# Queries of a head loaded one piece of work ahead into three tiles of each kind; operands of later stages made in a pool of four tiles

## The chip, the cores and the metric

One core of a Trainium2 chip. The metric is the device time of one execution of the whole program in microseconds (us), from one launch. TensorE (PE, with its weight loads PEld) multiplies, VectorE (DVE), ScalarE (ACT) and GpSimd (POOL) do the element-wise work, and SyncE (SP) issues every DMA of this kernel, in the order of its queue.

## What is computed

One layer on 2048 tokens of width 1024: a projection to queries, keys and values, two kinds of attention (8 heads with a forgetting gate over all earlier keys, 8 heads over a band of nine chunks of 64 tokens with a learned bias), an output product, a layer norm, a feed-forward block with a causal convolution, and a second norm. Cut to what matters here:

```python
def token_mixer(x, w_in, b_forget, rel_bias, w_out):
    proj = x @ w_in
    q_a, k_a, v_a, f_a, q_b, k_b, v_b = jnp.split(proj, SPLITS, axis=-1)
    log_f = jax.nn.log_sigmoid(f_a + b_forget).transpose(0, 2, 1)
    y_a = forgetting_attention(split_heads(q_a, 8), split_heads(k_a, 8), split_heads(v_a, 8), log_f)
    y_b = chunked_band_attention(split_heads(q_b, 8), split_heads(k_b, 8), split_heads(v_b, 8), rel_bias)
    y = jnp.concatenate([y_a, y_b], axis=1).transpose(0, 2, 1, 3).reshape(b, s, D_MIX)
    return y @ w_out

def reference(x, ...):
    x = layer_norm(ALPHA * x + token_mixer(x, w_in, b_forget, rel_bias, w_out), ln1_g, ln1_b)
    return layer_norm(ALPHA * x + conv_ffn(x, w_up, conv_w, conv_b, w_down), ln2_g, ln2_b)
```

All inputs are float32. The kernel keeps that precision by splitting an operand into a high part in the fast matmul format (`hi`) and a remainder (`lo`) and doing three matmuls for each product (`mm3`, lines 184 to 186).

## The kernel before

**Order.** The kernel is written against a tile framework: the Python code emits instructions in a program order, and a scheduler then places them on the engines, by that order as priority and by its own idea of when operands are ready. Every engine runs its list strictly in order, SP too: a DMA whose wait is not over holds all DMAs behind it.

**Stages.** First the projection alone (`projection`, products accumulated in `acc`, lines 184 to 186; call this dense work). Then attention and the rest of the projection woven together (`weave`): after each attention step, dense units are emitted in a fixed ratio. Before a pair of heads `p` is started, `ready(p)` emits dense units until its group of projections is complete. There are two attention passes, tokens 0 to 1023 (`chunks` 0 and 1) and tokens 1024 to 2047 (chunks 2 and 3); the dense work goes on with the output product of the first tokens. The rest, the feed-forward products, follows.

**Attention.** A piece of work is (pair of heads p, head s, chunk c of 512 queries), 32 in each pass, 64 in all. `start(n)` loads its keys (`load_keys`: tiles `ka`, `kb`, `vv`) and returns the generator `maxima`, whose first act before the change is to load the queries: `qa` (pool `a_q`, 2 buffers) and one of the two fixed tiles `qb0`, `qb1` (list `QB`), three DMAs (lines 552 to 554). `maxima` multiplies queries by keys (`sc`, line 574), DVE reduces each product to a row maximum (lines 577 and 582), and the maxima go back into row 96 of `qb` (line 592, ACT). `logits` then multiplies again (`st`, lines 611 and 612), ACT takes the exponential (`pt`, line 623), POOL adds up the rows (line 632), and `weigh` multiplies by the values (`y`, line 698). `sc` and `st` have two PSUM banks each. In the loop over work, item i's logits are interleaved with item i+1's maxima: `start(i + 1)` is called at the top of item i.

**Operands of later stages.** `prepare_weights` makes hi and lo parts of `w_out` (16 operands, `wo_d`) and of seven sums or differences of blocks of `w_down` for each of 11 row blocks (77 operands, `wd_d`; 55 of them combine two blocks), and stores them to DRAM for later. It is a generator that `dense_work` advances one step every `PRE` = 9 dense units, from unit 60 on. Before the change a group first loads its four source blocks (`w_raw0` to `w_raw3`, one buffer each), then makes its operands one by one in one tile `w_hl` (both parts, one buffer): DVE combines into the lo half where two blocks are needed (line 279), ACT copies the hi part (line 177), DVE subtracts (line 180), one DMA stores both parts, 512 KB (line 282). The next operand may write `w_hl` only when that store has landed.

## Time and profile before

| what | value |
|---|---|
| times of three runs | 2785.5, 2792.08 and 12486.5 us; median 2792.08 us |
| profiled execution | 2789.79 us, span 2788.0 us from the first to the last instruction |
| PE busy | 2724.5 us, 98% of the span, 12632 matmuls |
| DVE, ACT, POOL busy | 1941.7, 1160.7, 623.2 us (70%, 42%, 22%) |
| mean granted clock of PE | 0.993 |
| bytes moved by DMA | 527.40 MB |

How to read it: a stretch is limited by the engine that is never idle there, and what a change can give is found in the idle time of that engine, and in what ended it. Granted clock 1.0 is the 2.4 GHz level, 0.5 the 1.2 GHz one; a value between them is the mean over a stretch in which both occurred. The third run above (12486.5 us) is far from the other two.

### The profile page before, as it was taken

The page shows a single profiled execution, that of the slowest core. Times are in us where ns is not written, and L with a number is a line of the kernel's source. Part 1 is how long each engine was busy: PE and PEld are TensorE (multiplying, and loading weights), DVE is VectorE, ACT ScalarE, POOL GpSimd, SP SyncE. Part 2 cuts the span into 40 slices and gives each one's busy share as a digit, 9 for nine tenths or more (in the row PEclk, how much of TensorE's full clock was granted, in tenths as well). Part 3 has the DMA queues.
Part 4 walks back from the last instruction along what each step waited for, and adds up shares of the span by engine and source line. Part 5 has one row for each costly group of instructions (what it writes and reads, how often), then busy time and mean ns, then how long its engine had stood idle before and what let it go on. Part 6 is the DMA issues. An engine that isn't in the chain of part 4 may idle for free.

```text
span 2788.0 us, 38642 instructions
## 1 busy us (share of the span) xinstructions
PE 2724.5 (98%) x12632; PEld 2045.3 (73%) x12632; DVE 1941.7 (70%) x3577; ACT 1160.7 (42%) x2004; POOL 623.2 (22%) x754
## 2 busy tenths in 40 slices
PE   9999999999999999999998999999999999999998
PEld 7676767675666656766786888888887788888886
DVE  4557576777677655668568888876568877777559
ACT  4434444444444443433225555553222555544221
POOL 2235242327567555333000000000000000000000
PEclk9999999999999999999999999999999999999999
DMA  8666767665455444677894444428778222236974
GB/s 242 197 207 196 228 194 229 211 201 169 144 182 182 137 144 153 199 198 217 293 328 142 141 166 156 155 83 311 260 247 322 87 80 81 78 88 206 323 227 161
DMA packets 324618, 527.40 MB, mean 189 GB/s; under 512 B 70688, under 2 KB 86176, under 8 KB 324416
## 3 DMA queue, kind: packets, MB, share of 16 engines
q1 hardware_dynamic: 324416, 524.93, 59.1%
q8 instruction: 100, 1.64, 0.2%
q14 instruction: 102, 0.84, 0.1%
HBM read 362.65 MB, written 162.14 MB: 188 GB/s over the span
## 4 chain that ended last, share of the span: by engine, by line
PE 84%; DVE 4%; DMA 4%; ACT 1%; issue 1%; POOL 0%; SPq 0%; DVEq 0%; ACTq 0%; POOLq 0%
PE acc L184 21%; PE acc L186 21%; PE acc L185 21%; PE y L698 8%; PE st L611 4%; PE sc L574 4%; PE st L612 3%; DMA qb<-qh_d 1%; PE sc L650 1%; DVE slot L180 1%; DVE slot L1132 1%; DMA slot<-in_w_v_dram 1%; DMA wd_d<-w_hl 1%; PE acc L841 0%; DVE slot L816 0%
## 5 line engine op out<-in xcount | busy, mean ns | idle before, releaser
L184 PE MATMUL acc<-slot,slot 128*128 128x512 f32 (+2 forms) x3064 | 1165.7, 381 | 17.9 <-ACT slot L177 17.9
L186 PE MATMUL acc<-slot,slot 128*128 128x512 f32 (+2 forms) x3064 | 1160.5, 379 | 6.6 <-DVE slot L180 6.6
L185 PE MATMUL acc<-slot,slot 128*128 128x512 f32 (+2 forms) x3064 | 1161.3, 379 | 0.0
L177 ACT ACTIVATE slot<-slot 128x512 fp32r<-128x512 f32 (+1 forms) x680 | 416.4, 626 | 674.2 <-DVE slot L1121 193.0
L184 PEld LDWEIGHTS acc<-slot,slot 128*128 128x128 f32 x3064 | 580.4, 189 | 135.9 <-ACT slot L177 23.5
L186 PEld LDWEIGHTS acc<-slot,slot 128*128 128x128 f32 x3064 | 579.7, 189 | 126.2 <-DVE slot L180 10.8
L185 PEld LDWEIGHTS acc<-slot,slot 128*128 128x128 f32 x3064 | 580.4, 189 | 112.6 <-issue 2.8
L180 DVE TENSOR_TENSOR slot<-slot,slot 128x512 fp32r<-128x512 f32 (+1 forms) x652 | 450.7, 707 | 194.4 <-ACT slot L177 167.9
L632 POOL TENSOR_TENSOR sums<-sums,pt 128x512 f32<-128x512 f32 (+3 forms) x416 | 426.0, 1024 | 251.9 <-ACT pt L623 189.0
L623 ACT ACTIVATE pt<-st 128x512 f32<-128x512 f32 (+3 forms) x544 | 261.7, 492 | 333.4 <-PE st L612 121.4
L698 PE MATMUL y<-pt,vv 128*64 128x512 f32 (+3 forms) x1088 | 281.6, 505 | 0.2 <-DVE yt L640 0.2
L611 PE MATMUL st<-qa,ka 128*128 128x512 f32 (+2 forms) x544 | 209.0, 385 | 9.0 <-ACT pt L623 8.5
L574 PE MATMUL sc<-kb,qb 66*128 66x512 f32 (+2 forms) x544 | 186.6, 373 | 10.8 <-DMA qb<-qh_d 8.1
L612 PE MATMUL st<-qb,kb 97*128 97x512 f32 (+2 forms) x544 | 189.9, 357 | 4.4 <-ACT qb L592 3.9
L577 DVE TENSOR_REDUCE mx<-sc 128x1 f32<-128x512 f32 x192 | 127.9, 686 | 80.0 <-PE sc L574 78.3
L611 PEld LDWEIGHTS st<-qa,ka 128*128 128x128 f32 x544 | 103.0, 189 | 96.0 <-issue 44.1
L698 PEld LDWEIGHTS y<-pt,vv 128*64 128x64 f32 x1088 | 82.0, 136 | 124.2 <-issue 111.5
L574 PEld LDWEIGHTS sc<-kb,qb 66*128 66x128 f32 x544 | 99.5, 190 | 78.6 <-DVE mx L582 17.5
L856 DVE SCALAR_TENSOR_TENSOR v<-u,cw,v 128x1024 f32<-128x1024 f32 x88 | 113.0, 1285 | 62.4 <-ACT v L855 44.2
L1005 POOL COPY u<-halo 128x2 f32<-128x2 f32 x44 | 17.6, 401 | 620.8 <-DVE v L857 620.8
L582 DVE CUSTOM_DVE_ANT_0 junk<-sc,bq 128x512 bf16<-128x512 f32 (+2 forms) x224 | 108.2, 483 | 49.4 <-PE sc L574 40.2
L632 POOL TENSOR_TENSOR sums<-pt 128x384 f32<-128x384 f32 (+1 forms) x64 | 79.5, 1243 | 255.4 <-PE sc L650 181.4
(116 smaller groups left out, 2250.3 us busy)
## 6 DMA issues: line engine op xcount, KB each, us to landing
slot<-wd_d SPq DMA_DIRECT2D x308, 256.0 KB
slot<-in_w_up_dram SPq DMA_DIRECT2D x176, 256.0 KB
wd_d<-w_hl SPq DMA_DIRECT2D x77, 512.0 KB
slot<-wo_d SPq DMA_DIRECT2D x128, 256.0 KB
h_d<-v SPq DMA_DIRECT2D x44, 512.0 KB
slot<-h_d SPq DMA_DIRECT2D x88, 256.0 KB
slot<-in_w_qk_dram SPq DMA_DIRECT2D x66, 256.0 KB
xq_d<-slot SPq DMA_DIRECT2D x56, 256.0 KB
```

Of the source, the lines that this page charges most:

```text
L177: nc.scalar.activation(hi, src, AF.Copy)
L180: lo_eng.tensor_tensor(lo, src, f32(hi), op=ALU.subtract)
L184: nc.tensor.matmul(acc, wh, mh, start=first, stop=False, **more)
L185: nc.tensor.matmul(acc, wh, ml, start=False, stop=False, **more)
L186: nc.tensor.matmul(acc, wl, mh, start=False, stop=last, **more)
L574: nc.tensor.matmul(sc[:, m0:m1], qb[:KR, tq], kb[:KR, m0:m1], start=True, stop=True)
L577: nc.vector.tensor_reduce(m, sc[:, k0:k1], axis=AX.X, op=ALU.max)
L611: nc.tensor.matmul(st[:, w2], ka[:, js], qa[:, w2], start=True, stop=False)
L612: nc.tensor.matmul(st[:, w2], kb[:KM, js], qb[:KM, w2], start=False, stop=True)
L623: nc.scalar.activation(pt[:, w], st[:, w], AF.Exp)
L632: nc.gpsimd.tensor_tensor(acc[:, w], (acc if first is None else first)[:, w], pt[:, w], op=ALU.add)
L698: nc.tensor.matmul(y[half, w], v, pt[:, w], start=first and n < 2, stop=last and n >= len(tiles) - 2)
```

## The change

Queries are loaded by a function of their own, `load_queries(n)`, called in `start` for work n and for work n+1, so for one piece ahead; `qa` has three buffers and there are three `qb` tiles, taken in turn by n. `load_queries` calls `ready` too, so the projections of a group of heads are completed one piece of work earlier. `prepare_weights` loses its four source tiles and `w_hl`. It now takes an operand at a time: load into `w_lo` (2 buffers), load a second block into `w_v` (1 buffer) where there is one, a `yield`, combine in place, ACT copies hi to `w_hi` (1 buffer), DVE subtracts in place, two stores of 256 KB, a `yield`. Source blocks that several operands use are loaded once for each. `PRE` goes from 9 to 5, since an operand now takes two steps.

```diff
-PRE0, PRE = 60, 9
+PRE0, PRE = 60, 5
...
-        def parts(dst, u, v=None, op=None):
-            hl = tl(pool, [P, 2, CH], F32R, "w_hl")
+        def rows(src, i, j):
+            return src[i * P : i * P + P, CH * j : CH * j + CH]
+
+        def operand(dst, u, v=None, op=None):
+            lo, hi = tl(pool, [P, CH], F32, "w_lo", 2), tl(pool, [P, CH], F32R, "w_hi")
+            nc.sync.dma_start(lo, u)
             if v is not None:
-                src = f32(hl[:, 1])
-                nc.vector.tensor_tensor(src, u, v, op=op)
-                u = src
-            split(hl[:, 0], hl[:, 1], u, nc.scalar, nc.vector)
-            nc.sync.dma_start(dst.rearrange("l p m -> p l m"), f32(hl))
...
+                tmp = tl(pool, [P, CH], F32, "w_v")
+                nc.sync.dma_start(tmp, v)
             yield
...
+            if v is not None:
+                nc.vector.tensor_tensor(lo, lo, tmp, op=op)
+            split(hi, lo, lo, nc.scalar, nc.vector)
+            nc.sync.dma_start(dst[0], f32(hi))
+            nc.sync.dma_start(dst[1], lo)
+            yield
...
-        yp, pp, sm, qp = pool("a_y", 1), pool("a_p", 4), pool("a_sm", 4), pool("a_q", 2)
+        yp, pp, sm, qp = pool("a_y", 1), pool("a_p", 4), pool("a_sm", 4), pool("a_q", 3)
...
-        for n in range(2):
+        for n in range(3):
             t = tl(cst, [P, CH], F32R, f"qb{n}")
...
-        def maxima(p, s, c, head, qs):
+        def load_queries(n):
+            p, s, c = work[n]
+            ready(p)
...
             qa = tl(qp, [P, CH], F32R, "qa")
-            qb = QB[steps % 2]
-            steps += 1
+            qb = QB[n % len(QB)]
             nc.sync.dma_start(f32(qa[0:HD]), ql_d[p, hs, cs])
             nc.sync.dma_start(f32(qa[HD:P]), qh_d[p, hs, cs])
             nc.sync.dma_start(f32(qb[0:HD]), qh_d[p, hs, cs])
-            qs += [qa, qb]
+            queries[n] = qa, qb
...
-            qs = []
-            return head[s], qs, maxima(p, s, c, head[s], qs)
+            for k in (n, n + 1):
+                if k < len(work) and k not in queries:
+                    load_queries(k)
+            qs = queries.pop(n)
+            return head[s], qs, maxima(p, s, c, head[s], qs[1])
```

The line numbers move a little: the three matmuls of attention, 574, 611 and 612 before, stand at 572, 609 and 610 after, the value product 698 at 699; 184 to 186 and 177 to 180 stay. What the scheduler makes of it, at three places:

**PE, seventh piece of the second pass** (queries in `qb_962` before, in `qb_975` after). Before, the first product with the new queries stands right behind a value product:

```order
L186 MATMUL acc<-slot_7583,slot_5237 128x256
L698 MATMUL y<-pt,vv 64x512
L574 MATMUL sc<-kb_956,qb_962 128x512
L574 MATMUL sc<-kb_959,qb_962 128x512
L698 MATMUL y<-pt,vv 64x384
```

and after, behind the transposes that end the maxima of the piece ahead:

```order
L186 MATMUL acc<-slot_7787,slot_5305 128x256
L589 MATMUL sc<-ident_r,nm 1x128 x4
L609 MATMUL st<-qa,ka 128x512
L572 MATMUL sc<-kb_969,qb_975 128x512
L184 MATMUL acc<-slot_7787,slot_5310 128x256
L185 MATMUL acc<-slot_7788,slot_5310 128x256
L610 MATMUL st<-qb_981,kb_957 128x512
```

The maxima of one piece now follow those of the last without a gap in the list, with dense rows and logits of the piece in work (`qb_981`) between them.

**PE, where the second attention pass begins** (its first queries are in `qb_962` before, in `qb_975` after). Before, dense rows stand between the first products:

```order
L650 MATMUL sc<-sums,ones 64x512 x2
L574 MATMUL sc<-kb_941,qb_962 128x512
L611 MATMUL st<-qa,ka 128x512
L184 MATMUL acc<-slot_5194,slot_6747 128x512
L185 MATMUL acc<-slot_5195,slot_6747 128x512
L574 MATMUL sc<-kb_944,qb_962 128x512
L186 MATMUL acc<-slot_5194,slot_6748 128x512
L611 MATMUL st<-qa,ka 128x512
```

After, a long dense stretch ends there, and the first piece's twelve products (three key tiles for each of four query blocks) stand together:

```order
L186 MATMUL acc<-slot_5310,slot_6918 128x512
L609 MATMUL st<-qa,ka 128x512
L572 MATMUL sc<-kb_954,qb_975 128x512
L572 MATMUL sc<-kb_957,qb_975 128x512
L609 MATMUL st<-qa,ka 128x512
L572 MATMUL sc<-kb_960,qb_975 128x256
L572 MATMUL sc<-kb_954,qb_975 128x512
L572 MATMUL sc<-kb_957,qb_975 128x512
L572 MATMUL sc<-kb_960,qb_975 128x256
L572 MATMUL sc<-kb_954,qb_975 128x512
L572 MATMUL sc<-kb_957,qb_975 128x512
L572 MATMUL sc<-kb_960,qb_975 128x384
```

No dense row (184 to 186) follows for 61 matmuls. Over the whole attention part, the lists hold three stretches of 40 to 42 matmuls without a dense one before, and nine stretches of 31 to 91 after (431 matmuls in all, against 124).

**SP, the operands of later stages, in the middle of the second pass.** Before, four source blocks are loaded together, and one store belongs to an operand:

```order
L282 DMA wd_d<-w_hl 128x2x512
L523 DMA vv<-v_d 128x256
L400 DMA v_d<-slot_8174 128x4x64
L288 DMA w_raw_8581<-in_w_down_dram 128x512
L288 DMA w_raw_8583<-in_w_down_dram 128x512
L288 DMA w_raw_8585<-in_w_down_dram 128x512
L288 DMA w_raw_8587<-in_w_down_dram 128x512
```

After, a load or two and two stores belong to each operand (queries of the piece ahead, `qb_975`, and a key tile, `kb_954`, stand a few rows above):

```order
L547 DMA qb_975<-qh_d 64x512
L517 DMA ka<-kh_d 64x512
L518 DMA ka<-kl_d 64x512
L510 DMA kb_954<-kh_d 64x512
L512 DMA kb_954<-cum_d 2x512
L288 DMA wd_d<-w_hi 128x512
L519 DMA vv<-v_d 128x256
L289 DMA wd_d<-w_lo 128x512
L280 DMA w_lo<-in_w_down_dram 128x512
L396 DMA v_d<-slot_8382 128x4x64
L283 DMA w_v<-in_w_down_dram 128x512
```

The lists of the feed-forward stages hold the same matmuls in the same number as before.

## Rows read from the trace of the kernel before

**Rows 1.** The page: span, and busy time of the engines.

```profile
span 2788.0 us, 38642 instructions
...
PE 2724.5 (98%) x12632; PEld 2045.3 (73%) x12632; DVE 1941.7 (70%) x3577; ACT 1160.7 (42%) x2004; POOL 623.2 (22%) x754
```

**Rows 2.** Busy time by stage: stretch, length, PE, PEld, DVE, ACT, POOL, clock, DMA.

```profile
75.00:1340.00 1265.00, 1236.16 (x6114) 839.65 (x6114) 827.09 (x1972) 534.72 (x1058) 561.68 (x590) 0.99 0.62 188
...
1510.00:2720.00 1210.00, 1204.39 (x5203) 974.99 (x5202) 897.53 (x1223) 527.26 (x776) 43.90 (x124) 1.00 0.54 176
```

**Rows 3.** PE's waits, 60 to 1340 us: total, times, longest.

```profile
PE st L611 <- ACT pt L623: 8.5, 9, 2.1
PE sc L574 <- DMA qb<-qh_d: 8.1, 8, 2.1
PE st L612 <- ACT qb L592: 3.9, 3, 2.8
...
PE sc L574 <- DVE mx L582: 2.4, 2, 1.2
```

**Rows 4.** Timeline at one such wait: start, length, engine, instruction, idle before.

```profile
752.61 0.55 SPq L554 DMA_DIRECT2D qb<-qh_d  x1
...
758.52 0.73 PE L574 MATMUL sc<-kb,qb 66*128 66x512 f32 x2 [2.13 <-DMA qb<-qh_d]
```

**Rows 5.** Stretches of 5 us around the two longest such waits, as rows 2.

```profile
115.00:120.00 5.00, 5.00 (x15) 2.75 (x15) 2.69 (x9) 0.38 (x1) 0.72 (x1) 0.66 0.57 184
...
760.00:765.00 5.00, 5.00 (x24) 4.31 (x23) 2.71 (x7) 2.63 (x5) 1.49 (x2) 0.66 0.26 80
```

**Rows 6.** The chain that ended last, near 1000 us: start, length, what.

```profile
996.45 3.05 DMA wd_d<-w_hl
...
1000.75 0.39 PE st L611
```

**Rows 7.** ACT's waits for DMAs, 60 to 1340 us (ten rows).

```profile
ACT slot L177 <- DMA slot<-in_w_qk_dram: 20.0, 15, 3.3
...
ACT w_hl L177 <- DMA wd_d<-w_hl: 9.6, 10, 2.7
...
ACT w_hl L177 <- DMA wo_d<-w_hl: 4.3, 4, 2.2
...
ACT w_hl L177 <- DMA qh_d<-slot: 2.0, 1, 2.0
...
ACT slot L177 <- DMA qh_d<-slot: 1.2, 2, 0.6
```

**Rows 8.** DVE's waits for DMAs, 60 to 1340 us (four rows).

```profile
DVE w_hl L279 <- DMA wd_d<-w_hl: 18.3, 15, 3.4
...
DVE w_hl L279 <- DMA w_raw<-in_w_down_dram: 3.3, 3, 1.7
```

**Rows 9.** SP's own waits: total, times, longest.

```profile
SPq L552 <- PE st L612: 64.6, 31, 7.9
```

**Rows 10.** Groups of DVE, 75 to 1340 us: count, busy, mean ns, idle before.

```profile
L577 DVE TENSOR_REDUCE mx<-sc 128x1 f32<-128x512 f32 x192 | 127.9, 686 | 80.0 <-PE sc L574 78.3
...
L582 DVE CUSTOM_DVE_ANT_0 junk<-sc,causal_w 128x512 bf16<-128x512 f32 x32 | 21.8, 683 | 0.5 <-PE sc L574 0.2
```

**Rows 11.** PE's four waits where the second pass begins, 580 to 616 us.

```profile
PE sc L650 <- POOL sums L632: 1.4, 1, 1.4
...
PE y L698 <- DVE yt L640: 0.2, 1, 0.2
```

**Rows 12.** PE's waits in a stretch without dense work, 335 to 350 us.

```profile
PE st L611 <- ACT pt L623: 0.6, 1, 0.6
```

**Rows 13.** DMA issues of the operands: duration of the issue (ns), first and last.

```profile
L282 SPq DMA_DIRECT2D wd_d<-w_hl x77: 359/377/1182, 208.5 to 1020.1; - x77
...
L288 SPq DMA_DIRECT2D w_raw<-in_w_down_dram x44: 327/430/1148, 176.6 to 957.7; - x44
```

**Rows 14.** The page: DMA issues by line, count and size.

```profile
slot<-in_w_qk_dram SPq DMA_DIRECT2D x66, 256.0 KB
```

More of the change, by code (lines that the diff above doesn't have):

```diff
@@ L500, in attention @@
         loads = 0
-        steps = 0
+        queries = {}
         zeros = set()
@@ L554, in maxima @@
             nc.sync.dma_start(f32(qb[0:HD]), qh_d[p, hs, cs])
-            qs += [qa, qb]
+            queries[n] = qa, qb
+        def maxima(p, s, c, head, qb):
+            fox = p < 4
+            KR = HD + 2
             seg = c + 1 if fox else min(c + 1, 2)
```

25 lines of the change are left out of this document (6 added, 19 removed).

## Prediction, made before the changed kernel ran

> **What bounds the kernel now.** I read the page first: PE is busy for 2724.5 us of a span of 2788.0, so 63.5 us of idle PE are all that better order can give [rows 1]. By stage, 1236.16 of the 1265 us between 75 and 1340 us are PE's, which leaves 28.8 us idle in the stretch in which attention and projection are woven; from 1510 to 2720 us it is 5.6 us [rows 2]. The change touches nothing behind the weave, so its whole account lies in those 28.8 us, and in what the clock costs beside them. Next I read who ended PE's waits there: the exponentials on ACT for 8.5 us, the queries' load into `qb` for 8.1 in eight waits, the row of maxima that ACT writes into `qb` for 3.9, a DVE reduction for 2.4 [rows 3]. The reader is to see two kinds: PE waits on a DMA itself, or on ACT or DVE, which were late.
>
> The timeline shows the first kind at its worst. SP issues the load of `qb` at 752.61; PE runs out of other work, waits 2.13 us, and starts with the new queries at 758.52, 5.9 us behind the issue [rows 4]. The five microseconds behind it have a granted clock of 0.66, so about two thirds of them ran at 1.2 GHz instead of 2.4, and PE lost 1.7 us (0.34 x 5) while it counts as busy; the same 0.66 stands from 115 us on, behind another of the eight [rows 5].
>
> The second kind shows in the chain. A store of `w_hl` takes 3.05 us to land, ACT holds its next operand back for it, an exponential is queued behind that, and PE gets on with the product behind it at 1000.75, 4.3 us after the issue [rows 6]. Such waits on DMAs add up to 72.7 us on ACT (ten rows) [rows 7] and 27.4 on DVE (four rows) [rows 8]: 100 us, for which PE waited at most 14.8 us on these two engines (8.5 + 3.9 + 2.4) [rows 3]. So about 15% of a wait of ACT or DVE reaches PE.
>
> All sums are against the profiled execution, 2789.8 us; the median of the runs shown is 2.3 us above it.
>
> **Queries one piece ahead.** The three DMAs and their bytes stay; they are emitted one piece earlier. SP still holds them until the piece before last has done its last product with the tile: that wait, 64.6 us in 31 times, concerns the same event as before [rows 9], and SP's queue behind it stalls as it did. But the first reader comes one piece later, 1265 us / 64 pieces, some 20 us, against 5.9 us from issue to use at the worst place. I take the 8.1 us as gone, and the two stretches of low clock with them: **-8.1 and -3.4**. The bounds: nothing gained, and this sum.
>
> What is late next: with `qb` there, the products may start as soon as the keys are, and the scheduler lets them follow the last maxima directly, as the rows of order show. Keys are now the last thing to land. The trace of before has no wait of PE for `kb`. Between 0 and the 8.1 us that `qb` cost I take **+2**, nearer to none, since the keys stand a few issues ahead of where the queries stood.
>
> **Dense work bunched.** `ready` is called a piece earlier, and PE's list has 431 matmuls in stretches without dense rows against 124. Where the second pass begins, twelve products with two PSUM banks stand together, so DVE's reductions set the pace: eight of 686 ns and, on the diagonal, four of 683 ns at most, 5.5 to 8.2 us and say 7.4 [rows 10], of which PE's own part is 12 x 0.235 = 2.8 (a 512-column dense product about every 0.23 us: 1204.39 us / 5203 in the later stage [rows 2]). The first two need not wait. That is 4 us of idle PE. Then PE waits for the maxima to come back into `qb` (2.8 us at the longest [rows 3]; products of the next piece hide part: 1), perhaps for the load of `qb` itself (0 to 2.1, the longest of the eight waits [rows 3]: 1), and the clock falls once (1.7 [rows 5]). That is 7.7 us; what PE waited there before, 3.1 us in four waits [rows 11], goes: **+4.5**, between 0 and +9. The other eight dense-free stretches have 370 matmuls; in the three of before, 124 matmuls, PE waited for ACT in one, 0.6 us [rows 12]; by their number that is 1.8, so **+2**, between 0 and +8 (8.5 us is all that PE waited for ACT's exponentials [rows 3]). Elsewhere bunching costs nothing, since PE is busy with the one or the other; if that cover went, it would be priced like these stretches.
>
> **Operands of later stages.** 153 DMAs (60 loads, 93 stores) become 334 (148 loads, 186 stores): 181 issues more at 0.38 to 0.43 us [rows 13], 69 to 78 us of SP up to 1020 us. SP is off the path while its loads are early, so this costs nothing directly; it delays what queues behind, and the price is in the waits below. The 88 loads more bring 23 MB, a tenth of what the stretch moves (188 GB/s x 1265 us = 238 MB); the DMA engines are busy 0.62 of it, so they have room [rows 2]. ACT's and DVE's instructions are the same in number (93 copies, 93 subtractions, 55 combinations).
>
> Removed: the waits for the one `w_hl` to be stored, 9.6 + 4.3 on ACT [rows 7] and 18.3 on DVE, and 3.3 for the source blocks [rows 8], with a 2.0 of ACT between: 37.5 us, of which 15% reach PE: -5.6. Added: waits for loads that now stand one operand ahead instead of up to four. Nearest is the weight load of the projection, which is split soon after its issue: 20.0 us [rows 7] for 66 loads [rows 14], 0.30 us each. 148 loads at that price are 45 us, 15% of it 6.7. Waits for `w_hi` to be stored I put at a fifth of those removed, 0.5. Together **+1.5**. The bounds: none of the new waits (-5.6), or every one straight to PE (+39).
>
> The Trainium skill, in "DMA: Bandwidth & Descriptors", section "Bandwidth", says to batch DMAs to 1 MiB or more, and in its fit gives every transfer a fixed 2.0 us beside its bytes at 436 GB/s: by it a 512 KB store would be an estimated 3.2 us and each of two halves 2.6, which speaks against this change. The 3.05 us of the store agree with the page [rows 6]; no row of before has its half.
>
> **The sum.** -8.1 - 3.4 + 2 + 4.5 + 2 + 1.5 = -1.5, so 2788.3 us on the profiled execution's 2789.8: I forecast **2788**, no change that counts. What the queries give is taken back where dense work is bunched.
>
> **The rivals.**
> First, slower: ACT is held by loads. Its place is the copy to `w_hi` (line 177) ahead of exponentials in ACT's list, with two `st` banks behind it. For it speaks that this path is on the chain already [rows 6]; against it, that only 15% of such waits arrive. At 148 loads x 0.30 us = 45 us, all of it reaching PE, less 11.5 for the queries and 5.6: 2818. It decides from the point where ACT's waits pass on more than a quarter (11 us). Over 2% (2846) it would take 0.5 us for each load, all at PE.
>
> Second, faster: the bunching is hidden, keys are early and the new waits are few: -11.5 - 5.6 = -17, 2773; with half of PE's 14.8 us on ACT and DVE gone too, 2765.
>
> Third, the change does not do what it says: SP's queue, longer by 181 issues and held 64.6 us by these very loads [rows 9], brings the queries no earlier. Then 2789.8 + 4.5 + 2 + 1.5 = 2798.
>
> Fourth, hidden slack: if busy PE is not PE at its peak, more than 63.5 us could go, and the time fall below 2734. Against it speaks that the later stage runs 5203 matmuls in 1204 us with hardly any wait [rows 2]. The Trainium skill, in "Trainium Kernel Development and Optimization", section "Performance Expectations", calls matmul busy time a bad measure of distance from peak, because matmuls are pipelined, and wants that of weight loads; by it the 73% of PEld would leave room [rows 1], but the change removes no matmul and no weight load.
>
> **How the numbers follow.** Forecast, 2778 to 2795: 0.5. Slower by held ACT, 2796 to 2845: 0.18, half of it below 2812; over 2% 0.02. Faster, 2752 to 2777: 0.18, most of it above 2770. Change without its effect, 2796 to 2805: 0.1. Hidden slack, below 2734: 0.01; the last 0.01 for a second pass that starves PE for longer (over 2%). The range 2770 to 2812 takes in the forecast, the third rival, half of the first and most of the second: 0.8. The forecast's own is 2778 to 2795. A measurement of this kernel can tell about 2% from no change (56 us), so faster 0.01, within 0.96, slower 0.03.
>
> **What would show it.** Right: no wait of PE for `qb` worth a microsecond outside the start of the second pass; there, a stretch with some 8 us of idle PE, ended by DVE's reductions; ACT waiting 30 to 60 us for `w_lo`; a granted clock near 0.993 again. Wrong: PE waits ended by `kb` of over 5 us, SP's waits for `w_hi` or `w_lo` with loads of weights or tokens late behind them, or PE's waits on ACT's exponentials of 15 us and more.

## The result and the profile after

The changed kernel takes 2828.18 us and the kernel before, run beside it, 2788.79 us, each the median of four runs. One run of each (3860.75 and 12486.5 us) is far from the others and stays out of the ratio, which compares 2823.07 to 2830.64 us with 2782.03 to 2792.08 us. The ratio is 1.0139, 95% interval 1.0118 to 1.0160: slower by 1.4%, some 39 us, where 2788 was forecast with a range up to 2812. It is less than the 2% below which a difference was to count as none, but the interval is well clear of 1.

The profiled execution took 2830.64 us. Its page answers to [rows 1]: the span is 40.7 us longer, PE is busy for 15.8 us more with the same 12632 matmuls, and idle for 24.9 us more. The mean granted clock is 0.983 (0.993 before), and the DMAs move 550.48 MB (527.40).

```profile
span 2828.7 us, 38901 instructions
...
PE 2740.3 (97%) x12632; PEld 2059.1 (73%) x12632; DVE 1938.2 (69%) x3579; ACT 1161.9 (41%) x2004; POOL 621.8 (22%) x754
```

The table by stage answers to [rows 2], columns as there. The later stage is the same to 0.01 us. The loss is all in the weave of attention and projection, which is 45 us longer by these rows; the stretch between the two rows is 5 us shorter.

```profile
75.00:1385.00 1310.00, 1256.49 (x6158) 858.01 (x6157) 826.06 (x1978) 537.09 (x1061) 559.94 (x590) 0.97 0.66 201
1550.00:2760.00 1210.00, 1204.40 (x5202) 974.96 (x5201) 897.68 (x1223) 527.89 (x777) 44.36 (x124) 1.00 0.54 176
```

PE's waits from 60 to 1380 us (total, times, longest) answer to [rows 3]. The eight waits for `qb` are gone, as forecast, and the key load costs 1.9 us. New is DVE: 23.5 us (12.3 + 6.4 + 4.8) for the reductions `mx` and `nm`, where 2.4 stood.

```profile
PE sc L572 <- DVE mx L575: 12.3, 10, 2.7
PE st L609 <- ACT pt L621: 7.1, 14, 1.2
PE sc L572 <- DVE mx L580: 6.4, 8, 3.9
...
PE sc L589 <- DVE nm L586: 4.8, 4, 1.6
PE st L609 <- DMA qa<-ql_d: 4.0, 1, 4.0
...
PE st L610 <- ACT qb L590: 2.1, 4, 0.9
PE sc L572 <- DMA kb<-kh_d: 1.9, 1, 1.9
```

DVE's waits for the operands' loads answer to [rows 8]: 51.9 us in these two rows, where 21.6 stood in its two (18.3 of them for the store of `w_hl`, 3.3 for loads).

```profile
DVE w_lo L286 <- DMA w_v<-in_w_down_dram: 34.6, 15, 5.0
...
DVE w_lo L286 <- DMA w_lo<-in_w_down_dram: 17.3, 6, 4.6
```

SP's own waits answer to [rows 9]: its list stands for 94.2 us before the store of `w_hi` and for 29.2 before that of `w_lo`, where the kernel before stood for 57.3 before its one store (last row); 72.5 us of waiting for the query tiles are about the 64.6 of before.

```profile
SPq L288 <- ACT w_hi L177: 94.2, 51, 8.7
SPq L545 <- PE st L610: 72.5, 24, 13.8
...
SPq L289 <- DVE w_lo L180: 29.2, 41, 4.1
```

```profile
SPq L282 <- DVE w_hl L180: 57.3, 28, 7.8
```

Where in the weave is the time lost? The first row below is 440 to 700 us of the kernel before, the second the same stretch of the changed one (columns as in [rows 2]). Before, PE is idle for 6.8 us there at full clock. After, it is idle for 23.6 us and the clock is 0.89, so up to 29 us (0.11 x 260) of full-speed work are missing too: 1120 matmuls instead of 1269.

```profile
440.00:700.00 260.00, 253.18 (x1269) 174.75 (x1268) 184.05 (x443) 120.05 (x239) 102.91 (x117) 1.00 0.67 201
```

```profile
440.00:700.00 260.00, 236.38 (x1120) 161.76 (x1118) 159.40 (x393) 98.56 (x202) 63.61 (x86) 0.89 0.70 210
```

Inside it, the start of the second pass shows low clock behind an idle gap. PE waits 4.03 us for `qa` at 673.62 and is busy for 1.30 us of five; for the next 15 us the granted clock is 0.50, the 1.2 GHz level.

```profile
670.00:675.00 5.00, 1.30 (x3) 0.93 (x4) 0.75 (x2) 0.22 (x1) 0.00 (x0) 0.93 0.77 193
675.00:680.00 5.00, 4.37 (x8) 1.76 (x7) 3.96 (x10) 0.00 (x0) 0.00 (x0) 0.50 0.87 213
680.00:685.00 5.00, 3.94 (x9) 1.76 (x9) 3.40 (x8) 0.38 (x1) 0.00 (x0) 0.50 1.08 250
685.00:690.00 5.00, 4.86 (x11) 2.94 (x11) 2.38 (x5) 2.71 (x6) 2.24 (x2) 0.50 0.33 121
```

### The profile page after: what moved, and what is told of

It reads as the page before. It is cut to its first block, busy times and chain, and to the rows that moved or that the text cites. A ratio compares the mean times of both kernels' runs of the same rounds, so it can differ in the third digit from the quotient of the medians.

```text
span 2828.7 us, 38901 instructions
## 1 busy us (share of the span) xinstructions
PE 2740.3 (97%) x12632; PEld 2059.1 (73%) x12632; DVE 1938.2 (69%) x3579; ACT 1161.9 (41%) x2004; POOL 621.8 (22%) x754
## 2 busy tenths in 40 slices
DMA packets 338778, 550.48 MB, mean 195 GB/s; under 512 B 73584, under 2 KB 89072, under 8 KB 338576
## 4 chain that ended last, share of the span: by engine, by line
PE 79%; DMA 8%; DVE 7%; ACT 3%; issue 2%; SPq 1%; POOL 1%; DVEq 0%; ACTq 0%; POOLq 0%
PE acc L186 20%; PE acc L185 20%; PE acc L184 20%; PE y L699 7%; PE st L609 4%; PE sc L572 3%; PE st L610 3%; DMA w_v<-in_w_down_dram 1%; PE sc L648 1%; DMA slot<-in_w_qk_dram 1%; DVE slot L180 1%; DMA w_lo<-in_w_down_dram 1%; DVE row L654 1%; DVE w_lo L180 1%; DVE slot L1133 1%
## 5 line engine op out<-in xcount | busy, mean ns | idle before, releaser
L699 PE MATMUL y<-pt,vv 128*64 128x512 f32 (+3 forms) x1088 | 272.6, 509 | 3.5 <-DVE yt L638 3.5
L572 PE MATMUL sc<-kb,qb 66*128 66x512 f32 (+2 forms) x544 | 195.4, 381 | 21.1 <-DVE mx L575 12.3
L572 PEld LDWEIGHTS sc<-kb,qb 66*128 66x128 f32 x544 | 105.9, 198 | 73.7 <-DVE mx L575 25.2
L654 DVE RECIPROCAL row<-row 128x128 f32<-128x128 f32 x128 | 117.0, 933 | 28.4 <-ACT row L650 28.2
```

What stands on the lines that cost most here:

```text
L572: nc.tensor.matmul(sc[:, m0:m1], qb[:KR, tq], kb[:KR, m0:m1], start=True, stop=True)
L654: nc.vector.reciprocal(part, part)
L699: nc.tensor.matmul(y[half, w], v, pt[:, w], start=first and n < 2, stop=last and n >= len(tiles) - 2)
```

## Experiments

Two theories stood at first. **A**: the new operands cost, because their loads stand too near their use and DVE is held by them. **B**: the earlier projection costs, because stretches without dense work starve PE. Below, a ratio is to the kernel before run on the same chip, with its 95% interval; "us" is the ratio's distance from 1 times 2788.

| kernel | median us | ratio | interval | us |
|---|---|---|---|---|
| changed kernel | 2828.18 | 1.0139 | 1.0118 to 1.0160 | +39 |
| e2_operands | 2843.44 | 1.0186 | 1.0149 to 1.0222 | +52 |
| c1_pt8 | 2789.31 | 0.9995 | 0.9978 to 1.0012 | -1 |
| e1_q_pt8 | 2767.34 | 0.9911 | 0.9880 to 0.9943 | -25 |
| e3_no_ready | 2816.24 | 1.0096 | 1.0062 to 1.0129 | +27 |
| e5_qn_pt8 | 2748.77 | 0.9873 | 0.9859 to 0.9888 | -35 |
| e6_ops_ahead | 2832.04 | 1.0169 | 1.0154 to 1.0184 | +47 |
| e7_two_stores | 2789.02 | 1.0010 | 1.0000 to 1.0019 | +3 |
| e8_late | 2800.42 | 1.0061 | 1.0045 to 1.0077 | +17 |
| d1_bytes | 2827.69 | 1.0154 | 1.0126 to 1.0181 | +43 |
| d2_issues | 2821.73 | 1.0132 | 1.0106 to 1.0157 | +37 |
| e10_one_block | 2806.81 | 1.0075 | 1.0051 to 1.0099 | +21 |
| e11_unforced | 2777.73 | 0.9971 | 0.9956 to 0.9987 | -8 |
| x1_ops_oldorder | 2834.97 | 1.0186 | 1.0162 to 1.0211 | +52 |
| x3_old_opsorder | 2837.07 | 1.0195 | 1.0170 to 1.0221 | +54 |
| x4_after_e1order | 2817.02 | 1.0120 | 1.0099 to 1.0141 | +33 |
| x2_e3_e5order | 2796.24 | 1.0045 | 1.0026 to 1.0064 | +13 |
| x5_after_act | 2824.32 | 1.0147 | 1.0132 to 1.0162 | +41 |
| x7_d2_oldorder | 2817.14 | 1.0124 | 1.0107 to 1.0141 | +35 |

### Which part of the change it is

**Operands alone.** The new `prepare_weights` and `PRE = 5` with the queries of before (two tiles, loaded in `maxima` at the piece's own start); against the changed kernel:

```
-            for k in (n, n + 1):
-                if k < len(work) and k not in queries:
-                    load_queries(k)
-            qs = queries.pop(n)
-            return head[s], qs, maxima(p, s, c, head[s], qs[1])
+            qs = []
+            return head[s], qs, maxima(p, s, c, head[s], qs)
```

> The operands' part of the change alone (the new preparation, one step every 5 units of dense work); queries, their two tiles and the early projection stay as before. Theory A (each operand's loads stand only half an operand ahead, DVE waits for them, the row maxima behind it are late, PE stalls and its clock falls): all of the loss is here, 2815 to 2835 us; DVE waits for w_lo and w_v 40 us or more, PE waits for DVE's reductions 15 us or more, the granted clock in the mean about 0.985. Theory B (the projection forced a piece earlier leaves stretches without dense work): no loss here, 2783 to 2797 us, PE waits for DVE below 6 us, whatever DVE waits for loads.

Measured 2843.44 us: more than the whole change loses. Theory B is out as the main cause. Theory A has the side, but not its time (2835 us at most) and not most of its signs. The granted clock is 0.985, as it said; but DVE waits 22.6 us for `w_lo` and `w_v` (8.5 + 14.1), not 40, and PE waits 12.3 us for DVE's reductions `mx` and `nm` (2.8 + 2.7 + 6.8), not 15, and 11.2 us for `qb`.

```profile
PE sc L570 <- DMA qb<-qh_d: 11.2, 15, 1.4
PE sc L587 <- DVE nm L584: 6.8, 6, 1.9
```

```profile
DVE w_lo L286 <- DMA w_v<-in_w_down_dram: 14.1, 8, 3.4
DVE w_lo L286 <- DMA w_lo<-in_w_down_dram: 8.5, 7, 4.1
```

**Queries alone.** The old `prepare_weights` with `PRE = 9`. It lacks the room for the third tiles, so two of the ten tiles for exponentials, 4 KB a partition, are given up (`PT = 8`), and the kernel before was run with 8 as well:

> The kernel before with 8 tiles for exponentials instead of 10, which frees the 4 KB a partition that the queries' part alone would lack. It only gives the price of those two tiles, to be taken off the next run. Both theories: within 6 us of the kernel before, 2786 to 2795 us, since four tiles make a group and the group is used four steps later.

> The queries' part of the change alone (loads a piece ahead, three tiles of each kind, the projection forced a piece earlier); operands are prepared as before; 8 tiles for exponentials. To be read against the kernel before with 8 tiles. Theory A: no loss, or a gain of up to 12 us against it (the waits for qb are gone). Theory B: all of the loss, 25 to 40 us above it, with the granted clock about 0.90 between 490 and 560 us and 0.80 between 630 and 700.

Two tiles fewer cost nothing (2789.31 us; the scheduler writes the very same lists). The queries' part alone gains 25 us. That is more than the 8.1 + 3.4 that the prediction counted, and the bunched dense work does not eat it up. The two parts alone come to 52 - 25 = 27 us, the whole change to 39; the three intervals reach 6 to 10 us each way, so it stays open whether the parts add.

**Without the early projection.** A piece whose group is not yet projected loads its queries at its own start:

```
             p, s, c = work[n]
-            ready(p)
...
-                if k < len(work) and k not in queries:
+                if k < len(work) and k not in queries and (k == n or work[k][0] // 2 == p // 2):
```

> The changed kernel, but queries are loaded a piece ahead only where their group of heads is already projected; the first piece of a group loads its own queries at its start, as in the kernel before, so the projection is never forced a piece earlier. Theory A: little comes back, 2815 to 2832 us, DVE's waits for w_lo and w_v stay at 45 us or more. Theory B: most of the loss comes back, 2785 to 2800 us, the stretch from 630 to 700 us has a granted clock above 0.9 again.

> The queries' part alone, as in the run e1_q_pt8 (2767 us), but without the early projection: a piece whose group is not yet projected loads its queries at its own start. The changed kernel gained 12 us from this (2828 to 2816). If the bunched dense work has a price of its own: 2750 to 2760 us. If it cost only because the late operands left DVE and SP no room: 2764 to 2772 us, no change.

With the new operands this returns 12 us (2816.24), with the old ones 11 (0.9911 to 0.9873). The intervals within each pair overlap or touch, but both pairs say the same: the early projection has a price of its own, about 11 us, and it is no part of the 52. The run with old operands and late projection, 2748.77 us, beats both kernels: 1.27% faster than before.

The table shows where each kernel falls behind: for the n-th product `st` of the trace (counted from 0), its start in the kernel before (us), and how much later it starts in others. The numbers are read off one profiled execution each.

```
n-th st    before   after    e2     e6     d2     x7     e7     e1     e5
  250       416.0   +14.5  +13.7  +14.7   -0.5   -1.1   +3.5   -3.1  -14.0
  300       502.4   +24.5  +27.0  +24.9   +6.8  +11.2   +2.6   -3.8  -18.4
  350       562.6   +34.7  +39.7  +30.9  +19.6  +13.7   +2.9   -0.2  -13.4
  400       640.4   +57.8  +55.2  +44.4  +31.2  +29.6   +2.9   +1.3  -12.7
  500       728.4   +65.8  +61.0  +48.8  +36.5  +29.2   +3.6   +2.9   -8.5
  800      1029.2   +53.3  +59.7  +43.7  +34.6  +28.5   +1.7  -10.3  -24.7
 1075      1322.6   +39.1  +55.6  +43.2  +30.8  +23.4   -0.7  -24.2  -41.7
```

Most of the loss, 41 us of 55 with the operands alone, falls between the 250th and the 400th `st`, 430 to 696 us of that run, though operands are made from 46 to 1062 us. Behind it the operands cost nothing, and the changed kernel wins back 27 us in the second pass (65.8 to 39.1) by its queries.

### What it is in the operands

**Loads a whole operand ahead.** The next operand's loads (`next(then)`) are issued before the current one's arithmetic and stores (`next(now)`), with three `w_lo` and two `w_v`:

```
+        now = None
+        for then in all_operands():
+            next(then)
+            yield
+            if now is not None:
+                next(now)
+                yield
+            now = then
```

> The operands' part alone, as in the run e2_operands (2843 us), but each operand's loads are issued a whole operand (10 units of dense work) before its arithmetic instead of half of one, with three tiles for the block and two for the second one. Theory A1 (the loads stand too near their use; where the projection is forced, 5 units are some 3.5 us of PE, shorter than a load): the loss goes, 2785 to 2803 us, DVE's waits for w_lo and w_v fall below 12 us, and the granted clock from 490 to 700 us is above 0.95. Theory A2 (the number of DMA issues on SP and its waits for two stores hold the queue, so that queries, keys and weights land late): the loss stays, 2825 to 2850 us, PE still waits 8 us or more for qb, SP's waits at the store of w_hi stay at 60 us or more.

2832.04 us: a gain of 5 us against e2 by ratio, with intervals that overlap. Twice the distance from load to use does not bring the time back, as theory A1 said that it would. But DVE's waits for the loads hardly fell either, to 19.6 us (13.6 + 6.0) from 22.6, where under 12 was expected, so this run alone does not show what those waits cost. Theory A2 has the time and not its signs: PE waits 5.8 us for `qb` and SP 44.2 us before the store of `w_hi`.

```profile
DVE w_lo L287 <- DMA w_v<-in_w_down_dram: 13.6, 10, 4.1
...
DVE w_lo L287 <- DMA w_lo<-in_w_down_dram: 6.0, 4, 2.2
```

**One store made two, no load more.** The kernel before, `w_hl` replaced by `w_lo` and `w_hi`, two stores of 256 KB for one of 512 KB:

> The kernel before with its own loads (four blocks at a time, shared by seven operands) and its own pace, but each operand in two tiles of 256 KB that are stored by two DMAs instead of one tile of 512 KB and one store: 93 issues more on SP, no load more. Theory A1: no loss, 2780 to 2797 us. Theory A2: a good part of the loss, 2810 to 2840 us, with SP waiting 60 us or more at the store of w_hi.

2789.02 us, 1.0010: 93 more issues that cost 0 to 5 us. The Trainium skill, in "DMA: Bandwidth & Descriptors", section "Bandwidth", says to batch DMAs to 1 MiB or more; the prediction weighed this against halving the stores. The measurement decides: nothing is lost here by halves.

**The extra loads by themselves.** The kernel before (`PT = 8`) with one load more at each of the 88 steps of `wd_d`, into two tiles that no engine reads, of 256 KB, or of 2 KB (`t[:1]` and one row of `w_down`):

```
+        def spare(k, n):
+            t = tl(pool, [P, CH], F32, "w_spare", 2)
+            r = HF * (n // 4) + k
+            nc.sync.dma_start(t, w_down[r * P : r * P + P, CH * (n % 2) : CH * (n % 2) + CH])
```

> The kernel before with 8 tiles for exponentials (2789 us), and 88 loads of 256 KB more: one at each of the 88 steps of the second kind of operands, into two tiles that no engine reads. They are the 88 loads (23 MB) by which the changed kernel exceeds the one before, with nobody waiting for them. Theory A3 (where the projection is forced the DMA engines are already nearly full, and 23 MB more make every queue entry land late): 2810 to 2840 us, with PE waiting over 8 us for qb. Theory A1 (DVE and ACT held by waits for their own operands): no change, 2785 to 2797 us. Theory A2 (SP's time for the issues): 2800 to 2825 us, and the same in the run d2_issues.

> As d1_bytes, but each of the 88 loads brings 2 KB (one partition) instead of 256 KB: the issue on SP and the place in the queue stay, the bytes go. Theory A3: no change against the kernel before, 2783 to 2795 us. Theory A2: most of what d1_bytes lost, 2800 to 2825 us. Theory A1: no change, as in d1_bytes.

This is the surprise of the study. 88 loads that no engine reads cost 37 us with 2 KB each, and 23 MB in them only 6 us more. (SP itself waits for such a load where the next one goes into the same tile: 4.7 us in d2, 20.9 in d1.) So most of the loss needs neither the bytes nor waits of DVE: the issues are enough; and yet 93 store issues more (e7) cost 3. Theory A2 is right for loads and wrong for stores.

**Fewer loads.** The operands alone, the second block not loaded (`tmp = lo`), which leaves out a part of the computation:

> The operands' part alone, as in the run e2_operands (2843 us), but the second block of a combined operand is not loaded: DVE combines the first block with itself, so 55 of the 148 loads (14.4 MB) go and DVE's, ACT's and the stores' work stays. This leaves out a part of the computation. Theory A3: the loss of 52 us shrinks by more than the share of bytes, to 5 to 30 us: 2795 to 2820. Theory A1 (waits of DVE for loads that stand near): it shrinks only by what DVE waited for the second block (14 us, a part of which reached PE): 2830 to 2843. Theory A2 (issues): 55 of 181 go, 2822 to 2832.

2806.81 us: 55 loads fewer return 31 of 52 us, more than A1 and A2 allowed and what A3 named; after d2 the bytes can't be the reason.

**Other places.** All steps behind the first pass (`PRE0, PRE = 644, 2`); and, without the early projection, no step while the projection is forced and one every 4 units otherwise:

> The changed kernel with all steps of the operands moved behind the first pass: first step at unit 644 of the dense work, one every 2 units, where pieces are long and PE never runs short (in the run e2_operands nothing was lost behind 700 us, though a third of the operands were made there). Theory A1: with 2 units between load and use and long pieces around it, the waits of DVE stay but they meet slack; 2760 to 2785 us. Theory A2: SP's queue is held as often, in less time; the loss moves into the second pass, 2815 to 2850 us.

> The changed kernel without the early projection (as in the run e3_no_ready, 2816 us), and with no step of the operands taken while the projection is forced; they follow one every 4 units of the woven dense work instead. Bytes, issues and arithmetic stay, only the place changes. Theory A3: the forced stretches lose their extra transfers, and most of the loss against the same kernel with the old operands (2749 us) goes: 2765 to 2790 us. Theory A1: the waits only move, 2805 to 2820 us. Theory A2: the issues only move, 2800 to 2820 us.

With all steps in the second pass the time, 2800.42 us, lies between the two theories, and the loss moves there: the 950th `st` starts 16.5 us earlier than in the kernel before, the 975th, some 50 us behind it, 4.4 us later. PE stands for 12.84 us of that in one wait, which ends at 1188.38 us, for a split on ACT, and the final loss is 17 us.

```profile
1188.38 0.80 PE L184 MATMUL acc<-slot,slot 128*128 128x512 f32 x1 [12.84 <-ACT slot L177]
```

With the same loads, bytes and arithmetic but no step in the forced stretches, 2777.73 us: 35 us below e3. So where the steps stand in the program, and how fast they follow, is worth 35 us with the same work in them.

### What the issues do: the order of SP's list

The scheduler writes each engine's list from the program's order and its own reckoning. Place by place, the traces of d2 and c1 differ in the kind or shape of 896 of 12632 matmuls, those of e7 and the kernel before in 705; d1 and d2 have the same order on PE, DVE and ACT. Is it the list of PE that costs, or the DMAs on the chip? To cross the two, PE's instructions up to the end of the attention were tied, by edges of order alone, into the order that the scheduler had written for another kernel:

```
+    for a, b in zip(order, order[1:]):
+        tc.add_manual_dep(pe[b], pe[a].name, kind, reason="order")
```

> The operands' part alone (as the run e2_operands, 2843 us), with PE's instructions up to the end of the attention tied into exactly the order in which the kernel before has them; all other engines are ordered by the scheduler around that. The loads, issues, stores and waits of the new operands all stay. Theory O (the new DMAs change the order that the scheduler writes for PE: from about 500 us on, some 60 matmuls of attention stand without dense work between them, and that costs, not the DMAs): 2785 to 2803 us. Theory R (the DMAs themselves cost on the chip: SP's issues, the queue, DVE's waits for loads): 2825 to 2850 us.

> The cross to x1_ops_oldorder: the kernel before with its own operands, loads and stores, but PE's instructions up to the end of the attention in exactly the order that the scheduler wrote for the operands' part alone. Theory O: slow without a single new DMA, 2822 to 2850 us, with a granted clock below 0.95 between 490 and 700 us. Theory R: 2783 to 2800 us, as the kernel before.

> The changed kernel, whole, with PE's instructions up to the end of the attention in the order of the run e1_q_pt8 (the queries' part alone, 2767 us). Theory O: 2765 to 2785 us, faster than the kernel before. Theory R: 2812 to 2832 us, as the changed kernel.

> The changed kernel without the early projection (as the run e3_no_ready, 2816 us), with PE's instructions up to the end of the attention in the order of the run e5_qn_pt8 (the same queries with the old operands, 2749 us). Theory O: 2748 to 2772 us. Theory R: 2802 to 2820 us.

Neither theory holds as it was put: the new operands lose 52 us in PE's old order, as theory R has it, and the old operands lose 54 us in the new one, as theory O has it; x4 came out as theory R, x2 between the two. But x1 says why, since PE cannot turn to other work there: of its waits for `qb`, one is 19.1 us long, near 495 us.

```profile
PE sc L570 <- DMA qb<-qh_d: 29.7, 11, 19.1
```

The same wait is 20.2 us in x2.

```profile
PE sc L571 <- DMA qb<-qh_d: 23.9, 4, 20.2
```

In x4, the third kernel that was tied to an order made for early queries, there is no such wait for it: PE's longest is 11.3 us, for ACT's split of a projection weight. What stands ahead of that load, and is it SP that is short?

> The changed kernel, whole, with one edit: the 148 loads of the operands are issued by ACT instead of SP. Their number, bytes, distance and readers stay, and the scheduler orders all engines anew. Theory S (SP's queue is what is short between 440 and 520 us, where 16 loads of tokens, operands, keys and queries all stand in it): most of the loss goes, 2755 to 2785 us, and PE's list has no stretch of 60 rows without dense work there. Theory R (the loads themselves cost, by the transfers and by what waits for them): 2805 to 2835 us, ACT's own issues added.

> The run d2_issues (88 loads of 2 KB that nobody reads, 2822 us), with PE's instructions up to the end of the attention in the order of the kernel before. Theory S on the chip (each issue takes SP's time, and what stands behind it lands late): the loss stays, 2808 to 2830 us, as a wait of PE for a load, since PE may not turn to other work. Theory S in the list alone (the scheduler reckons SP short and writes PE a worse order, though the chip's SP has the time): 2785 to 2798 us.

x7 has the 88 small loads and PE's old order, and loses 35 us as d2 does. Its timeline (start, length, engine and line, instruction, pieces; for PE the idle time before it) shows the place. SP issues the last six of 16 token loads, `in_xT`, from 468.88 on, and only then the queries; PE, which has done its dense rows, stands for 12.12 us. About 3.1 of the 6.17 us are a wait of SP: one of the six loads goes into a `slot` tile whose store to `kl_d` has not landed yet. The query load behind them waits for its turn alone.

```profile
468.88 6.17 SPq L327 DMA_DIRECT2D slot<-in_xT_dram  x6
475.09 0.45 SPq L561 DMA_DIRECT2D qa<-qh_d  x1
475.58 0.60 SPq L562 DMA_DIRECT2D qb<-qh_d  x1
```

```profile
467.86 0.39 PE L620 MATMUL st<-qb,kb 97*128 97x512 f32 x1
480.37 0.58 PE L582 MATMUL sc<-kb,qb 66*128 66x256 f32 x1 [12.12 <-DMA qb<-qh_d]
```

In the kernel before the same load stands ahead of 13 of these 16:

```profile
452.49 0.35 SPq L319 DMA_DIRECT2D slot<-in_xT_dram  x1
452.92 0.59 SPq L554 DMA_DIRECT2D qb<-qh_d  x1
...
457.99 3.92 SPq L319 DMA_DIRECT2D slot<-in_xT_dram  x5
```

And in the changed kernel, whose program asks for these queries a whole piece earlier, it stands behind all of them (the last twelve are shown) again:

```profile
484.94 9.15 SPq L315 DMA_DIRECT2D slot<-in_xT_dram  x12
494.14 0.45 SPq L546 DMA_DIRECT2D qa<-qh_d  x1
494.63 0.59 SPq L547 DMA_DIRECT2D qb<-qh_d  x1
```

It is the 25th load into a `qb`, that of the first piece of the seventh pair. SP's list around it, with a number for each row, in the kernel before and in the changed one:

```
462 L400 DMA v_d<-slot_5015 128x4x64
463 L319 DMA slot_5174<-in_xT_dram 128x512
464 L554 DMA qb_962<-qh_d 64x512
465 L400 DMA v_d<-slot_5047 128x4x64
466 L230 DMA slot_5083<-in_w_qk_dram 128x512
```

```
541 L280 DMA w_lo<-in_w_down_dram 128x512
542 L420 DMA kl_d<-slot_5213 128x512
543 L315 DMA slot_5242<-in_xT_dram 128x512
...
554 L315 DMA slot_5308<-in_xT_dram 128x512
555 L546 DMA qa<-qh_d 64x512
556 L547 DMA qb_975<-qh_d 64x512
```

The load moved from behind three token loads to behind the last. This can be counted for every kernel: how many of the 16 token loads of the second half stand ahead of it. Beside it stands the longest run of PE's rows without dense work from the 285th to the 320th `st` (none under 16 counted).

```
kernel            us   token loads ahead   longest run without dense rows
e5_qn_pt8        -35          2                    -
e1_q_pt8         -25          2                   36
e11_unforced      -8          1                   26
c1_pt8            -1          3                   16
before             0          3                   16
e7_two_stores     +3          2                   17
x2_e3_e5order    +13         16                    -  (tied to e5)
e8_late          +17          1                   24
e10_one_block    +21         16                   26
e3_no_ready      +27         16                   62
x4_after_e1order +33         16                   36  (tied to e1)
x7_d2_oldorder   +35         16                   16  (tied to before)
d2_issues        +37         16                   56
changed kernel   +39         16                   91
x5_after_act     +41          1                   20
d1_bytes         +43         16                   56
e6_ops_ahead     +47         16                   59
e2_operands      +52         16                   62
x1_ops_oldorder  +52         16                   16  (tied to before)
x3_old_opsorder  +54          2                   62  (tied to e2)
```

All six kernels that lose nothing or next to it have that load ahead of 13 or more token loads; of the fourteen that lose, all but three have it behind all 16. Where PE's list is free, the late queries go with a long stretch of attention without dense rows (56 to 91 of them, only 26 in e10), in which PE waits for DVE and ACT; where PE's list is tied to an order made for early queries, PE stands and waits (x1, x2 and x7 for the query load, x4 for a weight). Either costs idle time and then the clock. The three exceptions have their own places. e8 has no step of the operands in the first pass and loses nothing there. x3 was tied to an order that the scheduler had made for late queries, and runs the 62 rows though its queries are early. In x5 the loads are on ACT's list, the queries are early, and the loss comes another way: ACT is late with the exponentials (23.7 us against 7.1 in the changed kernel), DVE waits longer for the loads, and PE waits 11.9 us at once for a reduction.

```profile
PE st L609 <- ACT pt L621: 23.7, 17, 6.8
PE sc L572 <- DVE mx L575: 17.6, 6, 11.9
...
DVE w_lo L286 <- DMA w_lo<-in_w_down_dram: 36.2, 19, 5.2
```

The table has a limit. Its times are against the kernel before, and seven kernels with the new operands have the gain of the queries in them. Against the kernel with the same queries and the old operands (e1 with the early projection, e5 without), the new operands cost 64 us in the changed kernel, 62 in e3, 58 in x4, 48 in x2, 66 in x5, 42 in e8 and still 27 in e11. The query load is early in the last three, so a loss does not need a late one. What goes with the late load is the stretch from the 250th to the 350th `st`: there e2 loses 26 us, d2 20 and the changed kernel 17 against e1, while e8 and e11 lose nothing against e1 and e5; but x5 loses 12 there with an early load, and e10 only 4 with a late one.

So theory S's number for x5 (2755 to 2785) was missed by 40 us, though the query load did move ahead, and PE's list has no long run there. The Trainium skill, in "Trainium Kernel Development and Optimization", section "Key Constraints", says that DMAs issued from SP and from ACT run on the same DMA engines, and that issuing from several engines only saves the sequencer's issue time; x5 shows no gain from it, 1.0147 against 1.0139, though it does not test this alone, since ACT was late with its own work.

**What is shown and what is not.** Shown: the loss is the operands'; 88 issues of loads are enough for 37 us of it; with them the 25th load of queries is listed behind 16 token loads; and with PE's order held, PE waits 12 to 20 us for just that load in three kernels of four. Not shown: that this load is the cause of the loss in the changed kernel, where PE waits for no `qb` at all. Not tried: the changed kernel with only this load moved ahead again, which would show how much of the 52 us hangs on it alone. Open is why 93 stores do not upset the scheduler and 88 loads do. Open too is the rest of the operands' loss: about 14 us that e2, e6 and the changed kernel lose before the 250th `st` and d2 does not, and what d2 and x7 lose between the 350th and the 400th, 12 to 16 us. In x7 the trace shows there 10 us of idle PE, where the kernel before has 3, in waits of at most 2.8 us for DVE, ACT, POOL and `qb`, and a granted clock of 0.83 and 0.87 from 600 to 670 us (1.00 before).

## Why the prediction was wrong, point by point

**Queries (-8.1).** Right: no wait for `qb` is left in the changed kernel. The clock's share (-3.4) did not come: instead of two dips to 0.66 over 5 us there is a clock of 0.89 over 260 us. By itself the part gains more than was counted, 25 us, and 35 without the early projection, against a sum of -3 for it (-8.1 - 3.4 + 2 + 4.5 + 2). The gain was looked for in idle time alone; see the last section.

**Keys (+2).** Right: 1.9 us in one wait.

**Dense work bunched (+4.5 and +2).** Right in kind: the early projection costs 11 to 12 us in both pairs of kernels, against 6.5, within its bounds of 0 and 17. At the start of the second pass PE is idle for 8.0 us between 630 and 700 us (61.99 busy of 70), near the 8 that were named, but half of that is one wait for `qa` (4.0) and not DVE's reductions.

```profile
630.00:700.00 70.00, 61.99 (x198) 35.46 (x198) 40.12 (x75) 19.42 (x37) 15.15 (x14) 0.78 0.61 183
```

**Operands (+1.5; bounds -5.6 and +39).** This is the step that failed: put at +1.5, the operands alone measured +52 (e2), outside their bounds. The sum of waits was not far off: DVE waited 51.9 us for the loads and ACT 10.0 (6.3 + 3.7), 62 against 45, or 0.42 us for each load against 0.30.

```profile
ACT w_hi L177 <- DMA w_lo<-in_w_out_dram: 6.3, 3, 3.8
ACT w_hi L177 <- DMA w_lo<-in_w_down_dram: 3.7, 5, 1.8
```

In the chain of the changed kernel an operand's load takes 3.2 to 5.4 us to land, a store of a half 2.0 to 4.5. The prediction's estimate of 2.6 us for a half comes from a fit that the Trainium skill, in "DMA: Bandwidth & Descriptors", section "Anatomy of one DMA — SWDGE (gpsimd) path", gives for DMAs that GpSimd issues; SP issues these.

```profile
461.91 2.01 DMA wd_d<-w_hi
465.82 3.57 DMA w_lo<-in_w_down_dram
477.57 4.52 DMA wd_d<-w_hi
```

But most of the price needs none of these waits: d2 has none of the new ones on DVE and ACT and loses 37 us. Nor does the chain that ended last tell the price: from 60 to 1400 us the operands' loads stand in it for 69 us in the changed kernel and 54 in e11, which is faster than the kernel before, and for 3 in d2. The sentence that failed is the one before the waits: "SP is off the path while its loads are early, so this costs nothing directly; it delays what queues behind, and the price is in the waits below". Between 450 and 500 us SP is on the path, at the least in x1, x2 and x7, where PE's order is held. The operands' steps, the 16 token loads, keys, values and queries of the next pieces all stand in its one list, and 88 more entries change who stands behind whom. The prediction counted 181 issues at 0.38 to 0.43 us, 69 to 78 us of SP over 1000 us, and asked no further where they stand; 93 stores more cost next to nothing (e7), and 88 loads more 37 us (d2). It read how the change moves SP's rows in the second pass alone, and not near 450 us, where the order of `qb` and `in_xT` could have been seen. How the 52 us divide between the late query load and other places stays open: with the loads off SP's list (x5) the time did not come back.

**DMA engines have room.** Right: 23 MB more cost 6 us (d1 against d2, 0.22%).

**The rivals.** The first ended on the right side and near the right time (2818), by a mechanism that did not happen, so by luck: PE's waits for ACT's exponentials went down (7.1 from 8.5), and it was DVE's reductions that PE waited for (23.5 us from 2.4). The third named the right queue, longer by 181 issues, and then asked only whether it brings the queries no earlier. Most did come earlier, and no wait for `qb` was left; but the 25th load came later, and where the second pass begins PE waits 4.0 us for a `qa`. The second, faster, is what the queries' part does alone: 2767.34 us, between its 2773 and 2765.

**The signs.** Of those for "right", the missing waits for `qb` came true; the clock (0.983), and ACT's waits for `w_lo` (they were DVE's) did not. Of those for "wrong", one came true as it was put: SP waits for `w_hi` and `w_lo` (123 us in two rows) with loads of tokens late behind them, the last twelve issued from 484.94 us on, where the kernel before had issued its last at 475.79.

## What to carry to other kernels

Before pricing a change that adds DMAs, read the issuing queue's list at its busiest place, not its share of the span: find the load that is needed first, and see what stands ahead of it before and after. Where a scheduler writes the lists, entries that no engine reads can cost most of what real ones do (37 us against 52 here), so each part of a change should be timed alone: here one part was worth 25 us and the other cost 52. Keeping bulk loads that are needed late (tokens of the next half) behind small ones that are needed at once is the next thing to try; it was not tried here.

## What the runs showed of the hardware beside this

PE's busy time depends on the order of its matmuls. From the first to the last `st`, the kernel before takes 1250.3 us and e5_qn_pt8 1208.7, with the same 6063 matmuls, at a mean clock of 0.993 and 0.994; only 3.7 us of the 41.6 are idle time (26.7 to 23.0), so some 38 us went out of time that counts as busy. What changed is how often PE goes from one width of weights to another. Call narrow the products whose weights have 64 columns in the trace (`y`, and the sums' products with `ones`), and wide all others; from one start to the next, idle time left out:

```
in order                before: times, mean ns     e5_qn_pt8: times, mean ns
wide, then wide              4624, 186                  4670, 185
wide, then narrow             235, 293                   189, 292
narrow, then narrow           969, 206                  1015, 187
narrow, then wide             235, 400                   189, 404
```

Queries that are there early let the scheduler change less often between narrow and wide, 378 times instead of 470. By these means that is an estimated 14 us of the 38 (46 times 293 + 400 - 186 - 206 ns); that narrow follows narrow in 187 ns instead of 206 makes another 19. All changes between `y`, `sc`, `st` and dense are as many in both kernels, 1983 and 1992. The page of the faster kernel shows it as less busy time for the same matmuls, 37.7 us under [rows 1]; the prediction's fourth rival, slack inside PE's busy time, had hold of this, at a chance of 0.01 and for far more.

```profile
PE 2686.8 (98%) x12632; PEld 2042.2 (74%) x12632; DVE 1942.0 (71%) x3579; ACT 1161.9 (42%) x2004; POOL 621.7 (23%) x754
```

No run was made on the change of width itself, and the ends of matmuls are modelled in the profile, so short waits may stand in these means; the cause stays open.
